# A two-layer SSD / linear-attention / retention trunk on one core: the SSD skip written into the output tiles by ACT, and a newly planned order

## The chip, the cores and the metric

The kernel runs on one core of one Trainium2 chip. The metric is the device time of one execution in microseconds; the number to predict is the median of three executions.

## The reference

One sequence of 1024 tokens, width 1024, passes through two layers. Each layer projects the residual stream once and splits the columns among three token mixers; their gated outputs are concatenated, projected, normalised and gated. All in fp32; cut to what matters here:

```python
for i in range(DEPTH):
    u = h @ w_in[i]                       # 3376 columns: z, xbc, dt, gla q/k/v/g/a, ret q/k/v/g
    # A) SSD: depthwise conv + silu on x, B, C; 8 heads of 64, state 128, both directions
    y = bidirectional(scalar_decay_scan, C, B, x*dt_f, x*dt_b, la_f, la_b)
    y = y + d_skip[:, None] * x           # the skip, one factor per head
    y_ssd = rms_norm(y * silu(z), norm_w)
    y_gla = gla_branch(...)               # B) gated linear attention, 4 heads
    y_ret = retention_branch(...)         # C) retention, 4 heads, rotary
    mix = concat(y_ssd, y_gla, y_ret) @ w_out[i]
    h = layer_norm(ALPHA * h + mix)
    h = h + sigmoid(h @ w_pg[i] + b_pg[i]) * (p[i] @ w_pe[i])
```

## The kernel before

**Dense products.** Activations lie as channels x tokens, in two halves of 512 tokens. Every dense operand is split into a high and a low part (names ending in hi/lo, h/l), and every dense product is three matmuls, hi*hi, hi*lo and lo*hi: `pch` (a 128-channel projection of the inputs), `ptk` (a projection with tokens on partitions: 304 columns at the start of a layer, 256 for retention's values, the stage `rvs`), `pout` (output projection), `ppg` and `ppe` (gate and embedding). A split is one ACT copy and one DVE subtraction (`whi`/`wlo` of input weights, `khi`/`klo` of the later ones).

**The mixers** run in chunks of 128 tokens, eight per layer and group. SSD has two groups of four heads. For each group it first runs backward over the chunks (`weighted`, `advance`: POOL scales x into `xw`, PE makes the state product `pst`, POOL scales the state into `sq`, DVE adds). Then `front` makes a chunk's decay matrix M in a tile `E` (a DMA, eight ACT operations, a DVE select, an ACT exp, a DVE product with the scores `psg`) and `back` uses it: `psi` (state times C), `dT<-psi,dT` on DVE, `xd` on POOL (both directions added), `psy` (x times M), and DVE adds `psy` and `xd` into the output tile `yz`. The skip sits in M: `dd`, a diagonal matrix with the heads' factors, is made once per group on POOL and added to each chunk's M by DVE (`E<-E,dd`), so that `psy` contains the skip. GLA (`gla1`): `pgr`, `bk`, `gqm`, `pgs` (scores), `gks`, `pkt`, `pgn` (states), `pgo` (values). Retention: `prk`, `prn`, then `prs`, `pro`. `yssd` normalises the SSD output: `pss` (transposes), a chain of small DVE operations, `psr`. `lnorm` is the layer norm, whose results are `h1h`/`h1l`.

**What sets the order.** The program is recorded, not issued: every call becomes a node with its dependencies, and `Rec.order` plans all engines together with prices from `Rec.price`, picking at each step the candidate that can start first (ties by recorded place). `Rec.issue` then emits every instruction from one line, L522, so rows of the profile are told apart by tile names. A resource `port` is kept in the plan: a DVE operation with two SBUF operands (or in a fast form) and any POOL operation exclude each other. DVE operations named in `EITHER` may be given to POOL when enough of them are late. The recorded order, which is the priority, comes from `weave`: the chains of the mixers (`phases`) with independent projections (`FILL`) mixed in by `QUOTA`. `SHIFTS` adds random offsets to the priorities of stretches of nodes, 21 of them. `DP` and `DB` say by how many chunks a front runs ahead of its back; `LN0`/`LN1` how the layer norm is spread over the projections.

Of the kernel before, what the change touches and what calls it, by code (L numbers as in the profile page):

```python
# [45 lines left out]
LN0=(2,2,2)  # L46
LN1=(4,1,2)
# [11 lines left out]
Q_N = 34 + 8 * 6  # L59
# [15 lines left out]
SHIFTS = (  # L75
# [6 lines left out]
EITHER = ("wlo", "klo", "yl", "rW", "rz", "gsm", "gqm", "gsq", "rsq")  # L82
LOOK = 20.0
# [141 lines left out]
class Rec:  # L225
# [93 lines left out]
    def price(self, eng, fn, args, kw, kind):  # L319
# [18 lines left out]
        if eng == "ACT":  # L338
            aps = sum(isinstance(kw.get(k), View) for k in ("scale", "bias"))
            c = .08 + n * .00082 + (0 if ps else .035) + .085 * aps  # L340
            return c, c + .1, False
        tensors = [v for v in ins if v.size > 1 or n == 1]
        if eng == "DVE":
            two = len(tensors) > 1 and not ps
            fast = fn in ("tensor_scalar", "tensor_copy") and not ps
            aps = sum(v.size == 1 for v in ins) if n > 1 else 0
            c = .07 + n / (1920 if fast else 960) + .06 * aps
            return c, c + .085, two or fast
# [5 lines left out]
    def order(self, nodes):  # L354
# [64 lines left out]
        while left:  # L419
            best = None  # L420
            for e in engines:
                cand, queue = None, ready[e]
                if e == "POOL":
                    now = max(at[e], port)
                    late = [n for n in ready["DVE"] if est[n.i] <= now]
                    queue = sorted(queue + [n for n in late[2:] if n.alt], key=prio)
# [23 lines left out]
                if cand is not None and (best is None or cand[0] < best[0]):  # L450
                    best = (*cand, e)
# [4 lines left out]
            t, _, n, e = best  # L456
# [69 lines left out]
def trunk(ctx: ExitStack, tc: tile.TileContext, xT, pT, wch, wt1, wt2, wout, wpg, wpe,  # L526
# [55 lines left out]
    def tt(eng, o, a, b, op):  # L582
        eng.tensor_tensor(o, a, b, op)
# [20 lines left out]
    FILL = 'c01dk2K3rQgGH'  # L604
    QUOTA = ((6, 8), (8, 17), (17, 22), (24, 28), (29, 35), (36, 36), (40, 40))
# [4 lines left out]
    GO = 1  # L610
    QF = 1
    DB = 2
    DP = (1,1,1,1)
# [174 lines left out]
    for layer in range(DEPTH):  # L788
# [87 lines left out]
        def conv_group(g):  # L876
            X[g] = [sl.get("X", (P, 2, 256)) for _ in range(4)]
            for i in range(2):
                xo = yield from conv(4 * g + i, lambda half, own: own)
                for half in range(2):  # L880
                    ps = cxt("pxt", (P, 4, P))
                    for c in range(4):
                        o = half * HALF + c * P
                        PX.transpose(ps[:, c, :], xo[:, o:o + P], ident)
                    for j in range(2):
                        act.activation(X[g][half * 2 + j][:, :, i * P:i * P + P],
                                       ps[:, 2 * j:2 * j + 2, :], AF.Copy)
                yield
# [13 lines left out]
        def ssd(g, B, C, Bt):  # L902
# [13 lines left out]
            def advance(dst, src, c, d, xw):  # L916
# [15 lines left out]
            dd = sl.get("dd", (P, 4, P))  # L932
            tt(pool, dd[:], ident.unsqueeze(1).broadcast_to([P, 4, P]),
               vb[:, 32 + 4 * g:36 + 4 * g].unsqueeze(2).broadcast_to([P, 4, P]), ALU.mult)

            def front(c):
# [22 lines left out]
                tt(vec_, M, M, dd[:], ALU.add)  # L959
                return M, xw, dT  # L960

            def back(c, Mx):
                M, xw, dT = Mx
                half, o = c // 4, slice((c % 4) * P, (c % 4 + 1) * P)
                if c % 4 == 0:
                    for j in range(2):
                        yz[2 * g + j][half] = sl.get("yz")
# [28 lines left out]
                for j in range(2):  # L996
                    tt(vec_, yz[2 * g + j][half][:, o], psy[:, j, :], u[:, j, :], ALU.add)
# [5 lines left out]
            sl.put(Sf, dd)  # L1003
# [703 lines left out]
```

## Time and profile before

| | us |
|---|---|
| median of 3 executions (lowest, highest) | 1247.55 (1246.6, 1248.52) |
| the profiled execution's own time | 1249.67 |
| its span, first to last instruction | 1247.9 |
| PE busy in the span | 1219.0 (98%) |
| DVE busy | 929.4 (74%) |
| ACT busy | 585.9 (47%) |
| POOL busy | 204.0 (16%) |

The profiled execution took 2.1 us more than the median, and 1.8 us of its time lie outside the span. PE was granted its full clock almost throughout (0.997 on the mean). A PE row's length is modelled: a dense matmul's row lasts 0.39 us though the next one starts 0.23 us later, so a wait shorter than the difference leaves no idle time in the rows.

### The profile page before, as it was taken

How to read it: one execution, taken by the hardware profiler on the slowest of the kernel's cores; microseconds unless marked ns; L12 is line 12 of the kernel's file. 1: busy time of each engine (PE TensorE's matmuls, PEld its weight loads, DVE VectorE, ACT ScalarE, POOL GpSimd, SP SyncE). 2: the span in 40 equal slices, each digit the busy share in tenths (PEclk: the TensorE clock that was granted, in tenths of full speed). 3: DMA queues.
4: the chain of work that ended last, by engine and by line, in shares of the span. 5: the costliest groups of instructions: out<-in, count | busy, mean ns of one | idle time of the engine just before them, and what ended most of it. 6: DMA issues, size and time to landing. Idle time of an engine off the chain costs nothing. (4 is left out here: it accounts for less than half of the span.)

```text
span 1247.9 us, 19871 instructions
## 1 busy us (share of the span) xinstructions
PE 1219.0 (98%) x7120; PEld 1009.2 (81%) x7120; DVE 929.4 (74%) x1982; ACT 585.9 (47%) x1237; POOL 204.0 (16%) x201
## 2 busy tenths in 40 slices
PE   8999999999999999999999999999999999999998
PEld 7887888768888788788898877787798887888887
DVE  5579897788588967796626788878686889579862
ACT  5466766532222435364534756565322224355552
POOL 0025552001001300120000354631000002001000
PEclk9999999999999999999999999999899999999999
DMA  7134432112132796233101453220121315952341
GB/s 252 43 98 154 147 123 76 43 33 70 48 102 66 236 309 219 85 125 132 65 28 51 151 149 126 86 93 18 46 66 43 101 53 198 340 183 85 118 157 51
DMA packets 82584, 142.58 MB, mean 114 GB/s; under 512 B 10867, under 2 KB 17973, under 8 KB 82485
## 3 DMA queue, kind: packets, MB, share of 16 engines
q1 hardware_dynamic: 82484, 141.31, 35.5%
q8 instruction: 56, 0.92, 0.3%
q14 instruction: 44, 0.35, 0.1%
HBM read 116.89 MB, written 17.04 MB: 107 GB/s over the span
## 5 line engine op out<-in xcount | busy, mean ns | idle before, releaser
L522 PE MATMUL pch<-xh,whi 128*128 128x512 f32 x352 | 147.1, 418 | 1.2 <-DVE gS L522 1.2
L522 PE MATMUL pch<-h2h,whi 128*128 128x512 f32 x352 | 145.8, 414 | 0.5 <-DVE E L522 0.5
L522 PE MATMUL pch<-xh,wlo 128*128 128x512 f32 x352 | 138.0, 392 | 0.1
L522 PE MATMUL pch<-h2h,wlo 128*128 128x512 f32 x352 | 137.8, 391 | 0.0
L522 PE MATMUL pch<-xl,whi 128*128 128x512 f32 x352 | 137.5, 391 | 0.0
L522 PE MATMUL pch<-h2l,whi 128*128 128x512 f32 x352 | 137.5, 391 | 0.0
L522 ACT ACTIVATE khi<-kraw 128x512 fp32r<-128x512 f32 (+1 forms) x160 | 89.1, 583 | 84.6 <-DMA kraw<-in_wout 40.8
L522 PE MATMUL ppg<-h1l,khi 128*128 128x512 f32 (+1 forms) x264 | 101.4, 384 | 1.8 <-DVE h1l L522 1.8
L522 PE MATMUL ppg<-h1h,khi 128*128 128x512 f32 (+1 forms) x264 | 101.1, 384 | 0.0
L522 PE MATMUL pout<-yl,khi 128*128 128x512 f32 x256 | 99.8, 390 | 1.0 <-DVE yl L522 1.0
L522 PE MATMUL ppg<-h1h,klo 128*128 128x512 f32 (+1 forms) x264 | 100.7, 383 | 0.0
L522 PE MATMUL pout<-yh,khi 128*128 128x512 f32 x256 | 100.7, 393 | 0.0
L522 PE MATMUL pout<-yh,klo 128*128 128x512 f32 x256 | 99.9, 390 | 0.7 <-DVE klo L522 0.7
L522 DVE SCALAR_TENSOR_TENSOR cacc<-cu,hp,cacc 128x1024 f32<-128x1024 f32 x64 | 87.8, 1372 | 16.2 <-ACT cacc L522 15.5
L522 DVE TENSOR_TENSOR wlo<-raw,whi 128x512 fp32r<-128x512 f32 (+1 forms) x79 | 56.7, 721 | 43.1 <-ACT whi L522 42.7
L522 ACT ACTIVATE whi<-raw 128x512 fp32r<-128x512 f32 (+1 forms) x98 | 60.8, 623 | 59.2 <-PE pch L522 39.6
L522 POOL TENSOR_TENSOR klo<-kraw,khi 128x512 fp32r<-128x512 f32 (+1 forms) x27 | 37.6, 1399 | 301.3 <-ACT khi L522 196.0
L522 ACT ACTIVATE E<-E,ecu 128x128 f32<-128x128 f32 x256 | 79.8, 392 | 8.5 <-DMA E<-dcu 8.4
L522 DVE TENSOR_TENSOR klo<-kraw,khi 128x512 fp32r<-128x512 f32 (+1 forms) x101 | 61.2, 622 | 29.6 <-ACT khi L522 13.0
L522 POOL TENSOR_TENSOR wlo<-raw,whi 128x512 fp32r<-128x512 f32 (+1 forms) x19 | 30.2, 1590 | 306.6 <-ACT whi L522 288.7
L522 PEld LDWEIGHTS pch<-xh,whi 128*128 128x128 f32 x352 | 66.2, 188 | 16.2 <-issue 3.6
L522 PEld LDWEIGHTS pch<-h2h,whi 128*128 128x128 f32 x352 | 66.2, 188 | 15.7 <-issue 1.9
(283 smaller groups left out, 2872.1 us busy)
## 6 DMA issues: line engine op xcount, KB each, us to landing
raw<-in_wch SPq DMA_DIRECT2D x88, 256.0 KB, 2.8
E<-dcu SPq DMA_DIRECT2D x32, 512.0 KB, 4.1
kraw<-in_wout SPq DMA_DIRECT2D x64, 256.0 KB, 4.2
kraw<-in_wpg SPq DMA_DIRECT2D x64, 256.0 KB, 3.2
dT<-deu SPq DMA_DIRECT2D x64, 128.0 KB, 3.4
dlo<-klo SPq DMA_DIRECT2D x32, 256.0 KB, 2.5
klo<-dlo SPq DMA_DIRECT2D x32, 256.0 KB, 4.3
xraw<-in_xT SPq DMA_DIRECT2D x16, 256.0 KB, 4.7
```

Of the source, the lines that this page charges most:

```text
L522: getattr(self.real[n.eng], fn)(*map(real, args), **{k: real(x) for k, x in kw.items()})
```

## The change

1. `dd` and `E<-E,dd` are gone. At the end of `conv_group` ACT writes `d_skip * x` into the output tiles `yz`, 128x512 at a time with a per-channel factor (new columns of `par` from Q_D); in `back` DVE adds twice, first `u` (the tile `xd` or `dT`), then `psy`, each 128x128.
2. The planner: `SHIFTS` is empty; ties between candidates that can start at the same moment go to the one that could ask for the port first; POOL is offered an `EITHER` operation when three others are late, not two; `LOOK` is 22; ACT and DVE operations on 64 partitions are priced higher.
3. The recorded order: another `FILL`, `QUOTA`, `GO`, `DB`, `DP`, `LN0`, `LN1`.

```diff
-LN0=(2,2,2)
-LN1=(4,1,2)
+LN0 = (4, 1, 2) 
+LN1 = (4, 2, 4) 
-SHIFTS = (
...
+SHIFTS = ()
-LOOK = 20.0
+LOOK = 22.0
+            if o.pn == 64 and n >= 128:
+                c += .1
...
-                    queue = sorted(queue + [n for n in late[2:] if n.alt], key=prio)
+                    queue = sorted(queue + [n for n in late[3:] if n.alt], key=prio)
...
-                if cand is not None and (best is None or cand[0] < best[0]):
-                    best = (*cand, e)
+                if cand is not None:
+                    asked = max(at[e], est[cand[2].i]) if cand[2].port else cand[0]
+                    if best is None or (cand[0], asked) < best[:2]:
+                        best = (cand[0], asked, *cand[1:], e)
...
-    FILL = 'c01dk2K3rQgGH'
-    QUOTA = ((6, 8), (8, 17), (17, 22), (24, 28), (29, 35), (36, 36), (40, 40))
+    FILL = 'c01kd2r3KQHGg'
+    QUOTA = ((6, 8), (13, 17), (20, 22), (27, 28), (27, 36), (36, 36), (36, 40))
...
-    GO = 1
+    GO = 0
-    DB = 2
-    DP = (1,1,1,1)
+    DB = 1
+    DP = (1, 2, 1, 1)
...
+                    y = yz[2 * g + i][half] = sl.get("yz")
+                    act.activation(y[:], xo[:, half * HALF:(half + 1) * HALF], AF.Copy,
+                                   scale=pr[:, Q_D + 2 * g + i:Q_D + 2 * g + i + 1])
...
-            dd = sl.get("dd", (P, 4, P))
-            tt(pool, dd[:], ident.unsqueeze(1).broadcast_to([P, 4, P]),
-               vb[:, 32 + 4 * g:36 + 4 * g].unsqueeze(2).broadcast_to([P, 4, P]), ALU.mult)
...
-                tt(vec_, M, M, dd[:], ALU.add)
...
-                    tt(vec_, yz[2 * g + j][half][:, o], psy[:, j, :], u[:, j, :], ALU.add)
+                    y = yz[2 * g + j][half][:, o]
+                    tt(vec_, y, y, u[:, j, :], ALU.add)
+                    tt(vec_, y, y, psy[:, j, :], ALU.add)
```

The set of PE instructions is the same in both, kind by kind; nearly every row stands elsewhere. In three places the prediction rests on the new order.

DVE in the second layer's second SSD group, near its end, before: a chunk's M gets the diagonal before `psy` can use it, and one addition per half of the chunk's channels ends the chunk.

```order
L522 TENSOR_TENSOR dT<-psi,dT 128x512
L522 COPY_PREDICATED E<-mki,E 128x512
L522 TENSOR_TENSOR yz<-psy,xd 128x128 x2
L522 TENSOR_TENSOR E<-E,psg 128x512
L522 TENSOR_TENSOR Sf<-sq,pst 128x256
L522 TENSOR_TENSOR E<-E,dd 128x512
```

The same place after:

```order
L523 TENSOR_TENSOR dT<-psi,dT 128x512
L523 TENSOR_TENSOR E<-E,psg 128x512
L523 TENSOR_TENSOR yz<-yz,xd 128x128
L523 TENSOR_TENSOR Sf<-sq,pst 128x256
L523 TENSOR_TENSOR yz<-yz,psy 128x128
L523 TENSOR_TENSOR yz<-yz,xd 128x128
L523 COPY_PREDICATED E<-mki,E 128x512
L523 TENSOR_TENSOR yz<-yz,psy 128x128
```

The 128x512 addition is gone, and two 128x128 additions have become four, two of which read SBUF alone.

PE in the second layer's GLA stage before, in its longest piece without a dense matmul:

```order
L522 MATMUL pkt<-kc,gks 128x128 x2
L522 MATMUL pgs<-gqm,bk 128x256 x3
L522 MATMUL pgn<-gv,gkt 128x128 x2
L522 MATMUL pgs<-gqm,bk 128x256 x4
L522 MATMUL pgr<-kc,gla 128x129 x2
L522 MATMUL pgo<-gv,gA 64x64 x8
```

The same stage after; the `ptk` rows go on to a piece of eleven to thirteen such matmuls before the next `pgn`:

```order
L523 MATMUL pgn<-gv,gkt 128x128 x2
L523 MATMUL pgo<-gv,gA 64x64 x8
L523 MATMUL pgs<-gqm,bk 128x256 x3
L523 MATMUL pkt<-kc,gks 128x128 x2
L523 MATMUL pgs<-gqm,bk 128x256
L523 MATMUL ptk<-wlo,h2h 128x256
L523 MATMUL ptk<-whi,h2l 128x256 x2
L523 MATMUL ptk<-whi,h2h 128x256
```

The projection of retention's values, which stood behind the stage, is now cut up inside it.

POOL from the end of the second layer's SSD on, before:

```order
L522 TENSOR_TENSOR wlo<-raw,whi 128x512
L522 TENSOR_TENSOR sq<-Sf,tot 128x256
L522 TENSOR_TENSOR wlo<-raw,whi 128x512
L522 TENSOR_TENSOR xd<-dT 128x256
L522 TENSOR_TENSOR gqm<-bk,kc 128x256 x8
L522 TENSOR_TENSOR gsm<-gS,kc 128x256 x3
```

And after:

```order
L523 TENSOR_TENSOR sq<-Sf,tot 128x256 x2
L523 TENSOR_TENSOR xd<-dT 128x256
L523 TENSOR_TENSOR gqm<-bk,kc 128x256 x2
L523 TENSOR_TENSOR wlo<-raw,whi 128x512
L523 TENSOR_TENSOR gqm<-bk,kc 128x256 x14
L523 TENSOR_TENSOR wlo<-raw,whi 128x512
L523 TENSOR_TENSOR klo<-kraw,khi 128x512 x7
```

All sixteen `gqm` of the layer are POOL's now. Over the program POOL takes 21 more `gqm`, 25 more `klo` of 512 and 9 of 256 columns, 10 more `wlo` and 2 more `yl`, and 2 `gsm` less: 130 operations that either engine could have taken, where it had 65.

## Rows read from the trace of the kernel before

**Rows 1.** The page: the span, and busy time of each engine with its share.

```profile
span 1247.9 us, 19871 instructions
...
PE 1219.0 (98%) x7120; PEld 1009.2 (81%) x7120; DVE 929.4 (74%) x1982; ACT 585.9 (47%) x1237; POOL 204.0 (16%) x201
```

**Rows 2.** Busy time by stretch, in the order length, PE, PEld, DVE, ACT, POOL, then granted clock and DMA: SSD and GLA of the first layer, SSD and most of GLA of the second.

```profile
104.00:208.00 104.00, 103.25 (x622) 83.23 (x621) 95.78 (x165) 71.01 (x175) 52.87 (x56) 1.00 0.41 127
208.00:312.00 104.00, 99.94 (x638) 80.21 (x637) 80.67 (x238) 41.27 (x99) 8.46 (x8) 1.00 0.18 49
676.00:832.00 156.00, 150.68 (x840) 120.87 (x839) 129.96 (x209) 104.25 (x249) 71.01 (x73) 1.00 0.37 118
832.00:884.00 52.00, 50.14 (x331) 37.58 (x331) 40.07 (x133) 24.96 (x69) 5.62 (x9) 0.93 0.09 27
```

**Rows 3.** Waits of PE over the whole program: those of the gate products for `h1l` (total us, times, longest).

```profile
PE ppg L522 <- DVE h1l L522: 1.8, 2, 1.1
```

**Rows 4.** Timeline, PE around 205 to 208 us (start, length): two dense matmuls that follow each other, and `psi` between dense ones.

```profile
205.41 0.40 PE L522 MATMUL pch<-xh,whi 128*128 128x512 f32 x1
...
205.64 0.39 PE L522 MATMUL pch<-xl,whi 128*128 128x512 f32 x1
...
207.24 0.39 PE L522 MATMUL pch<-xh,wlo 128*128 128x512 f32 x1
...
207.46 0.60 PE L522 MATMUL psi<-Cch,Sf 128*128 128x128 f32 x4
...
208.14 0.40 PE L522 MATMUL pch<-xl,whi 128*128 128x512 f32 x1
```

**Rows 5.** Instructions of four tiles in each layer, with ns min/median/max and the starts of the first and the last: `pst` and `psy` bound SSD, `pgr` and `pgo` GLA.

```profile
L522 PE MATMUL pst<-xw,Btk x56: 377/378/483, 90.7 to 197.4; 128*128 128x256 f32 x56
...
L522 PE MATMUL pst<-xw,Btk x56: 377/379/483, 705.5 to 821.2; 128*128 128x256 f32 x56
...
L522 PE MATMUL psy<-E,X x128: 272/273/323, 110.8 to 202.1; 128*64 128x128 f32 x128
...
L522 PE MATMUL psy<-E,X x128: 272/273/324, 728.1 to 828.4; 128*64 128x128 f32 x128
...
L522 PE MATMUL pgr<-kc,gla x32: 271/275/378, 214.7 to 243.5; 128*128 128x129 f32 x32
...
L522 PE MATMUL pgr<-kc,gla x32: 272/275/378, 841.0 to 862.4; 128*128 128x129 f32 x32
...
L522 PE MATMUL pgo<-gv,gA x128: 222/222/271, 234.6 to 270.7; 128*64 128x64 f32 x128
...
L522 PE MATMUL pgo<-gv,gA x128: 222/222/369, 855.5 to 886.7; 128*64 128x64 f32 x128
```

**Rows 6.** Groups of DVE instructions (busy us, mean ns of one, then idle before and its releaser).

```profile
L522 DVE TENSOR_TENSOR E<-E,dd 128x512 f32<-128x512 f32 x32 | 25.1, 792 | 0.1
...
L522 DVE TENSOR_TENSOR E<-E,psg 128x512 f32<-128x512 f32 x32 | 21.6, 679 | 2.2 <-ACT E L522 1.5 <-PE psg L522 0.5
...
L522 DVE TENSOR_TENSOR yz<-psy,xd 128x128 f32<-128x128 f32 x48 | 12.1, 280 | 2.6 <-POOL xd L522 2.5
```

**Rows 7.** The same for ACT and POOL.

```profile
L522 ACT ACTIVATE gt<-gt,pr 128x512 f32<-128x512 f32 x31 | 22.1, 721 | 23.8 <-DVE gt L522 23.7
...
L522 POOL TENSOR_TENSOR xw<-X,wtab 128x256 f32<-128x256 f32 x56 | 54.6, 980 | 20.8 <-PE pst L522 12.2 <-DVE wtab L522 8.2
...
L522 POOL TENSOR_TENSOR gqm<-bk,kc 128x256 f32<-128x256 f32 x10 | 6.6, 668 | 52.6 <-DVE bk L522 46.4 <-PE pgn L522 6.1
```

**Rows 8.** Timeline around 776 to 780 us, second layer's SSD: POOL, DVE and PE (in brackets the idle time before and its releaser).

```profile
776.02 1.74 POOL L522 TENSOR_TENSOR wlo<-raw,whi 128x512 fp32r<-128x512 f32 x1
...
776.55 2.30 DVE L522 SCALAR_TENSOR_TENSOR cacc<-cu,hp,cacc 128x1024 f32<-128x1024 f32 x1
...
779.37 0.40 DVE L522 TENSOR_TENSOR Sf<-sq,pst 128x256 f32<-128x256 f32 x1
...
779.83 0.71 PE L522 MATMUL psi<-Cch,Sf 128*128 128x128 f32 x4 [1.37 <-DVE Sf L522]
```

**Rows 9.** Timeline around 514 to 518 us, where the first layer's gate products begin.

```profile
513.79 0.63 PE L522 MATMUL psr<-dg,ones_r 128*128 128x512 f32 x2
...
517.15 3.63 DVE L522 SCALAR_TENSOR_TENSOR h1l<-res,pr,h1h 128x512 fp32r<-128x512 f32 x3
517.16 2.41 POOL L522 TENSOR_TENSOR klo<-kraw,khi 128x256 fp32r<-128x256 f32 x2 [2.79 <-PE ppe L522]
518.49 0.50 PE L522 MATMUL ppg<-h1l,khi 128*128 128x512 f32 x1 [1.10 <-DVE h1l L522]
```

**Rows 10.** Timeline from 393 to 405 us, first layer, `yssd`, and in the last row the two `psr` behind it (ns min/median/max, then the starts of first and last).

```profile
393.42 0.29 PE L522 MATMUL pro<-rv,rA 128*64 128x64 f32 x4
393.54 0.29 PE L522 MATMUL pro<-rS,rW 128*64 128x64 f32 x4
...
395.15 0.66 PE L522 MATMUL pss<-kc,zacc 128*128 128x128 f32 x4
...
404.37 1.30 POOL L522 TENSOR_TENSOR wlo<-raw,whi 128x304 fp32r<-128x304 f32 x1 [17.87 <-DVE w1l L522]
...
404.88 1.33 DVE L522 TENSOR_TENSOR dg<-kc,rl 128x512 fp32r<-128x512 f32 x1
...
L522 PE MATMUL psr<-dg,ones_r x2: 398/434/470, 407.8 to 408.1; 128*128 128x512 f32 x2
```

More of the change, by code (lines that the diff above doesn't have):

```diff
@@ L58 @@
 Q_SNW, Q_GNW, Q_RNW, Q_RNB, Q_LNW, Q_LNB, Q_BPG, Q_CONV = 0, 4, 6, 8, 10, 18, 26, 34
-Q_N = 34 + 8 * 6
+Q_D = 34 + 8 * 6
+Q_N = Q_D + 4
 K_ID, K_LE, K_GT, K_LT, K_UGF, K_UGB = 0, 128, 256, 384, 512, 641
@@ L347, in price @@
             c = .07 + n / (1920 if fast else 960) + .06 * aps
+            if o.pn == 64 and n >= 128:
+                c += .08
             return c, c + .085, two or fast
@@ L455, in order @@
             assert best is not None, [(e, len(r)) for e, r in ready.items()]
-            t, _, n, e = best
+            t, _, _, n, e = best
             if e != n.eng:
@@ L964, in back @@
                 half, o = c // 4, slice((c % 4) * P, (c % 4 + 1) * P)
-                if c % 4 == 0:
-                    for j in range(2):
-                        yz[2 * g + j][half] = sl.get("yz")
                 if YO == 0:
@@ L1002, in ssd @@
             yield from pipelined(range(NC), front, back, DP[0])
-            sl.put(Sf, dd)
+            sl.put(Sf)
         g0 = run(conv_group(0))
@@ L1673 @@
         cols += [conv[:, c - C_X:c - C_X + P].T for c in CONV_COLS]
+        cols.append(chan(np.repeat(a["d_skip"][l], 64)))
         pars.append(np.concatenate(cols, axis=1))
```

6 rows, old and new, of the table SHIFTS are left out of this document.

## The prediction

> **What bounds the kernel now.** I read the page first: PE is busy for 1219.0 of 1247.9 us [rows 1]. That share says little of how well PE works, since a dense matmul's row lasts 0.39 us and the next starts 0.23 us after it [rows 4]. What it does say is that PE sets the time. Both kernels issue the same matmuls, kind by kind, so only two things on PE can change: what it costs to go from one kind of matmul to another, and the waits.
>
> The first is about nothing. From 207.24 to 208.14 stand two dense matmuls and four `psi` passes [rows 4]: 0.90 us. Two dense pitches are 2 x 0.227 = 0.45, which leaves 0.11 per pass, and that is what the longer runs of `psi` take too. The new order goes from dense to other matmuls 181 times instead of 171; I cost the ten at zero.
>
> So the waits remain. PE's idle time is 28.9 us. The start of the program and the evacuation behind the last matmul stay as they are. What lies between I place by stretch: PE idles 0.8 of 104 us in the first layer's SSD and 4.1 of 104 around its GLA, but 5.3 of 156 in the second layer's SSD and 1.9 of 52 in its GLA [rows 2]. In the same stretches DVE is busy 92%, 78%, 83% and 77%; in SSD it is the engine that comes right behind PE.
>
> Idle rows hide the start of each wait, so I compare the two layers by the clock. SSD, from the first `pst` to the last `psy`, takes 202.1 - 90.7 = 111.4 us in layer 1 and 828.4 - 705.5 = 122.9 in layer 2 [rows 5]. The second holds 12 more dense matmuls (2.7 us), 18 more `pla` of half the columns (2.1) and two more `psi` (0.4). The other 6.3 us are waits that the first layer doesn't have. GLA, from the first `pgr` to the last `pgo`: 56.0 us with 108 dense matmuls among them, and 45.7 with 48. Less the dense part, 31.5 against 34.8: 3.3 us of waits more.
>
> **What makes PE wait.** Two places in the timeline show the same pattern. At 776.02 POOL begins `wlo` (1.74 us); DVE's `cacc`, begun half a microsecond later, takes 2.30 us; `Sf` behind it on DVE is late, and PE stands for 1.37 us before `psi` [rows 8]. At 517.16 POOL begins two `klo` (2.41 us), DVE's three `h1l` take 3.63 us, and PE waits for them 1.10 us and once more, 1.8 in all [rows 3, 9]. A DVE operation with two SBUF operands waits while POOL works. One that reads PSUM doesn't: `E<-E,psg` takes 0.679 us, while `E<-E,dd`, on the same tile, takes 0.792 on the mean [rows 6].
>
> **The change, part by part.**
>
> *The skip, on DVE.* Removed: 32 `E<-E,dd`, 25.1 us [rows 6]. The 64 old additions become 64 that read PSUM (0.28 each, as before) and 64 that read SBUF alone. For these no row exists. Below: 64 x 0.28 = 17.9 us [rows 6]. Above: each also waits half a POOL operation, 0.49 us by `xw` [rows 7], in the half of SSD's time that POOL is busy (52.87 of 104, [rows 2]): 0.25 more, 33.9 us. I take what contention added to `E<-E,dd`, 0.792 - 0.679 = 0.11: 64 x 0.39 = 25 us. DVE gains nothing, between -7 and +9. The path to `psy` loses 0.79 us per chunk, and `psy`'s PSUM tile no longer waits for POOL's `xd`, on which DVE waited 2.5 us in all [rows 6].
>
> The Trainium skill ("SBUF — State Buffer", section "Who interferes with whom") states that a DVE instruction with two SBUF inputs contends with a GpSimd one that reads SBUF, and that whoever comes first blocks the other fully. Rows 8 and 9 agree. By that rule the new additions stand in the worst place, right behind `xd`; the upper end would hold, DVE would have 9 us more, and SSD's gain below would be gone.
>
> *The skip, on ACT.* 16 operations at 0.72 us, by `gt<-gt,pr`, which also takes a per-channel operand [rows 7]: 11.5 us. ACT is busy 68% in SSD [rows 2], and nothing but the far later additions waits for them. Cost nothing; if that cover were gone, at most 11.5 us.
>
> *SSD's order.* Both layers now have one and the same order there, with 306 dense matmuls between first `pst` and last `psy` (282 and 294 before) and no `pla`. Best case: layer 2 does as layer 1, -6.3. Worst: layer 1 does as layer 2, +6.3. I start from zero, as the rows give no sign, and take half the best case, -3, for the shorter chain and the added cover.
>
> *GLA's order.* The stage now holds 12 dense matmuls and 142 (layer 2: 118) `ptk` of half the columns, 12 x 0.227 + 142 x 0.114 = 18.9 us of cover (16.2 in layer 2). Layer 1 had 24.5 and hardly waited, layer 2 10.9. With 16.2 I expect layer 2 to lose most of its 3.3 us: -3, between 0 and -3.3. `gqm`, at 0.67 us on POOL [rows 7], leaves DVE, but holds up those of DVE's operations beside it that read SBUF alone; I cost it below.
>
> *The gate products.* From `psr` at 513.79 to the first `ppg` that needs `h1l`, at 518.49, layer 1 had 4.7 us, 1.1 of it waiting [rows 9]: too short for DVE's `res` and `h1l`. In the new order 54 dense matmuls stand between them, 12.3 us. The wait of 1.8, 2.2 with its hidden start, goes: -2.
>
> *The SSD norm.* From `pss` to `psr` layer 1 took 12.65 us for 48 dense matmuls and the four `pss` themselves, 11.3 us: 1.3 late; of the last `dg`'s 1.33 us, 0.8 lay beside POOL's `wlo`, which began before it [rows 10]. In the new order stand there, in both layers, 30 dense (6.8 us), 64 `pro`, which are 128 passes at 0.12 per four (3.8) [rows 10], one `prs`, four transposes of the next tile and the `pss`, 0.3 to 0.45 each group: 11.8 us. That is half a microsecond more than layer 1 had. Late by 0.8 twice if the conflict comes again, hardly if not, where it was 1.3 once: 0, between -1.3 and +0.5.
>
> *POOL's load.* It had 65 operations that DVE could have done, and rows 3 and 8 to 10 give 1.4 + 1.8 + 0.8 = 4 us of PE waits that they caused. With 130 at the same rate, +4. But more than half of the new ones are `klo`, in output projection and gate products, where the planned order now leaves room, and the planner's new tie rule places the port's conflicts where the chip has them. I take +2, between 0 and +4.
>
> **Sum.** -3 - 3 - 2 + 0 + 2 = -6. The profiled execution had 1249.67 (1247.9 of span and 1.8 outside), so 1243.7 against it; it was 2.1 above the median, and the forecast for the median is 1247.55 - 6 = 1241.5 us.
>
> **Rivals.**
>
> *The order without shuffles is worse.* The 21 shuffled stretches may have carried layer 1's smooth SSD. Then both layers run as layer 2 did: +6.3 in SSD, GLA unchanged, -2 and +2 as above: 1247.55 + 6.3 = 1254; half of it gives 1251. It decides once SSD in layer 1, less its dense matmuls and `pla`, takes more than about 50 us (111.4 - 64.0 - 0.7 = 47 now, 53 in layer 2). For it: nothing else explains why one stage differs so between layers. Against it: layer 2 lay inside the shuffled ranges too. Chance 0.12.
>
> *The port.* POOL's time grows by up to 21 x 0.67 + 35 x 1.74 + 9 x 1.2 = 86 us [rows 7 to 9], and each of the 64 new SBUF additions can be held up. If only a tenth of these 64, and as many of the 31 new `gqm` and `wlo`, end in a PE wait like that of rows 8 (1.4 us), that is 9 x 1.4 = 13 us against the 8 gained: 1252. It decides from six such waits on. The chance is from the rows, which show three such places for 65 operations: 0.12. The rule of the Trainium skill quoted above would have it wherever POOL comes first, and gives no rate.
>
> *Nothing moves.* Each wait gone is taken up by the next one, since DVE carries the same load in SSD (above): 1245 to 1250. Chance 0.16.
>
> *All waits in the mixers go.* Idle 12 us in the four stretches of [rows 2], some 16 with hidden starts; two thirds of it and the -2: 1235. Chance 0.12.
>
> *The forecast,* -2.5 to -9.5 us: 0.48.
>
> **Range and chances.** A change under 0.2%, 2.5 us, can't be told from none here. Faster 0.48 + 0.12 = 0.60, same 0.16, slower 0.24. The range from 1234 to 1252 leaves out the deeper part of the gain and the worse half of the two losses, some 0.2; the forecast's own is 1238 to 1245.
>
> **What would show it.** In the changed profile SSD of both layers should take about 306 x 0.227 + 47 to 49 = 116 to 118 us from first `pst` to last `psy`; GLA, less its cover, 31 to 32 us in both; no wait of `ppg` for `h1l` in layer 1. `yz<-yz,xd` should take 0.3 to 0.5 us, and `yz<-yz,psy` 0.28. The forecast is wrong if layer 1's SSD loses what layer 2's wins, or if PE's waits end at DVE operations stretched beside a POOL row.

## The result, and the profile after

The changed kernel took 1219.89 us (1219.69 to 1220.42), the kernel before beside it 1247.69: a ratio of 0.9777, 95% interval 0.9764 to 0.9789. That is 27.8 us less, where 6 were forecast. The sign was right; the time lies far below the range.

The page after, its span, busy times and granted clock:

```profile
span 1218.0 us, 19959 instructions
...
PE 1202.9 (99%) x7120; PEld 1006.3 (83%) x7120; DVE 917.0 (75%) x1949; ACT 591.0 (49%) x1253; POOL 264.3 (22%) x262
...
PEclk9999999999999999999999999999999999999999
```

Against [rows 1], PE is busy for 16.1 us less with the same 7120 rows, and idle for 15.1 us, where it was 28.9. So more than half of the gain isn't idle time in PE's rows.

All waits of PE that are left (total us, times, longest):

```profile
PE ptk L523 <- ACT xh L523: 6.1, 3, 4.7
PE pkt L523 <- DVE gks L523: 1.5, 4, 1.0
PE ppg L523 <- ACT gt L523: 0.9, 1, 0.9
PE prk L523 <- DVE rot L523: 0.8, 1, 0.8
PE pout L523 <- DVE yl L523: 0.7, 1, 0.7
```

The first is the start of the program. The wait for `h1l` of [rows 3] is gone. The last is of the kind of [rows 8, 9]: `yl` on DVE, 0.68 us at its median, takes 1.77 beside a `wlo` that POOL began half a microsecond earlier, and `pout` waits for it.

```profile
427.10 1.74 POOL L523 TENSOR_TENSOR wlo<-raw,whi 128x512 fp32r<-128x512 f32 x1
427.62 1.77 DVE L523 TENSOR_TENSOR yl<-glay,yh 128x512 fp32r<-128x512 f32 x1
429.44 0.50 PE L523 MATMUL pout<-yl,khi 128*128 128x512 f32 x1 [0.71 <-DVE yl L523]
```

Where did the time go? Between four marks both kernels do the same work: the first `pst` and the first `pout` of each layer. Before, `pout`, layer 1 and layer 2 (ns min/median/max, then starts of the first and the last):

```profile
L522 PE MATMUL pout<-yh,khi x128: 389/389/481, 420.0 to 511.7; 128*128 128x512 f32 x128
...
L522 PE MATMUL pout<-yh,khi x128: 389/389/494, 1040.4 to 1137.1; 128*128 128x512 f32 x128
```

After, `pst`, `psy`, `pgr`, `pgo` and `pout` of layer 1, then of layer 2:

```profile
L523 PE MATMUL pst<-xw,Btk x56: 377/378/483, 91.9 to 198.4; 128*128 128x256 f32 x56
...
L523 PE MATMUL psy<-E,X x128: 272/273/324, 109.7 to 205.4; 128*64 128x128 f32 x128
...
L523 PE MATMUL pgr<-kc,gla x32: 271/274/277, 229.3 to 262.2; 128*128 128x129 f32 x32
...
L523 PE MATMUL pgo<-gv,gA x128: 222/222/271, 239.8 to 276.2; 128*64 128x64 f32 x128
...
L523 PE MATMUL pout<-yh,khi x128: 388/389/481, 409.7 to 502.3; 128*128 128x512 f32 x128
...
L523 PE MATMUL pst<-xw,Btk x56: 377/378/483, 692.9 to 799.5; 128*128 128x256 f32 x56
...
L523 PE MATMUL psy<-E,X x128: 272/273/324, 710.7 to 806.4; 128*64 128x128 f32 x128
...
L523 PE MATMUL pgr<-kc,gla x32: 271/274/378, 830.4 to 863.5; 128*128 128x129 f32 x32
...
L523 PE MATMUL pgo<-gv,gA x128: 222/222/270, 840.9 to 875.6; 128*64 128x64 f32 x128
...
L523 PE MATMUL pout<-yh,khi x128: 389/389/481, 1010.8 to 1102.1; 128*128 128x512 f32 x128
```

With the `pst` starts of [rows 5]:

| stretch (same work in both) | before | after | |
|---|---|---|---|
| start to first `pst` | 90.7 | 91.9 | +1.2 |
| mixers of layer 1, `pst` to `pout` | 329.3 | 317.8 | -11.5 |
| output projection and gate, to the next `pst` | 285.5 | 283.2 | -2.3 |
| mixers of layer 2 | 334.9 | 317.9 | -17.0 |
| to the end | 207.5 | 207.2 | -0.3 |

Both layers' mixers now take the same time, and layer 1's, which I had taken as the smooth ones, lost 11.5 us. Inside the mixers I use the prediction's measure, a stage less its cover (0.227 us per dense matmul, 0.114 per half-width `ptk`, 0.12 per `pla`), and call it the stage's rest. SSD before: 46.7 and 53.3 us; after, with 306 dense matmuls in 113.5 us, 44.0 and 44.0. GLA before: 31.5 and 34.8; after 46.9 - 18.9 = 28.0 and 45.2 - 16.2 = 29.0. The measure leaves small kinds in the rest: before, eight `pga` (0.11 us each) stood in each layer's SSD stretch and now none does, and layer 1's has four `psi` more (0.11 each). So of the 2.7 and 9.3 us that SSD's rest lost, some 2.3 and 8.4 are SSD's own.

The same four stages by window (length; PE, PEld, DVE, ACT, POOL; clock; DMA), as [rows 2]: PE doesn't idle in SSD, and the clock is 1.00 everywhere; [rows 2] had 0.93 in layer 2's GLA.

```profile
91.90:205.40 113.50, 113.50 (x659) 92.57 (x657) 99.57 (x181) 80.37 (x200) 65.90 (x68) 1.00 0.42 127
229.30:276.20 46.90, 45.55 (x421) 38.66 (x422) 40.35 (x125) 24.27 (x72) 11.33 (x17) 1.00 0.09 24
692.90:806.40 113.50, 113.50 (x657) 92.38 (x657) 99.64 (x181) 80.07 (x199) 63.92 (x68) 1.00 0.42 127
830.40:875.60 45.20, 44.88 (x403) 37.11 (x401) 38.09 (x126) 24.41 (x73) 11.39 (x17) 1.00 0.09 25
```

The skip's own operations after, on DVE and ACT (busy us, mean ns, idle before), for [rows 6, 7]:

```profile
L523 DVE TENSOR_TENSOR yz<-yz,xd 128x128 f32<-128x128 f32 x48 | 18.4, 400 | 5.2 <-POOL xd L523 5.2
...
L523 DVE TENSOR_TENSOR yz<-yz,psy 128x128 f32<-128x128 f32 x64 | 16.6, 277 | 0.7
...
L523 DVE TENSOR_TENSOR yz<-yz,dT 128x128 f32<-128x128 f32 x16 | 5.9, 377 | 0.2
...
L523 ACT ACTIVATE yz<-cacc,pr 128x512 f32<-128x512 f32 x16 | 11.1, 716 | 1.5 <-DVE cacc L523 1.5
```

The mean of 400 ns hides two kinds: 34 of the 48 `yz<-yz,xd` took 0.30 us or less, the other 14 took 0.68 to 0.72. Each of the 14 began while a POOL operation was running, and ended 0.15 us after that operation's row. One of them, with its `sq`:

```profile
131.48 0.61 POOL L523 TENSOR_TENSOR sq<-Sf,tot 128x256 f32<-128x256 f32 x1
131.55 0.69 DVE L523 TENSOR_TENSOR yz<-yz,xd 128x128 f32<-128x128 f32 x1 [0.90 <-POOL xd L523]
```

### The profile page after: what moved, and what is told of

Read it like the earlier page. It is cut to its first block, busy times and chain, and to the rows that moved or that the text cites. A ratio compares the mean times of both kernels' runs of the same rounds, so it can differ in the third digit from the quotient of the medians.

```text
span 1218.0 us, 19959 instructions
## 1 busy us (share of the span) xinstructions
PE 1202.9 (99%) x7120; PEld 1006.3 (83%) x7120; DVE 917.0 (75%) x1949; ACT 591.0 (49%) x1253; POOL 264.3 (22%) x262
## 4 chain that ended last, share of the span: by engine, by line
PE 92%; DVE 5%; DMA 1%; issue 1%; ACT 1%; SPq 0%; DVEq 0%; ACTq 0%
PE pch L523 37%; PE ppg L523 14%; PE pout L523 13%; PE ptk L523 8%; PE ppe L523 4%; PE psi L523 2%; PE pst L523 2%; PE psy L523 2%; PE pro L523 1%; PE pgs L523 1%; PE prs L523 1%; DVE rt L523 1%; PE psg L523 1%; PE prn L523 1%; DVE gks L523 1%
## 5 line engine op out<-in xcount | busy, mean ns | idle before, releaser
L523 POOL TENSOR_TENSOR klo<-kraw,khi 128x512 fp32r<-128x512 f32 (+1 forms) x61 | 76.5, 1272 | 303.4 <-ACT khi L523 111.2
L523 POOL TENSOR_TENSOR wlo<-raw,whi 128x512 fp32r<-128x512 f32 (+1 forms) x29 | 44.7, 1546 | 365.9 <-ACT whi L523 271.2
L523 ACT ACTIVATE khi<-kraw 128x512 fp32r<-128x512 f32 x160 | 89.1, 582 | 54.9 <-DMA kraw<-in_wout 26.5
L523 DVE SCALAR_TENSOR_TENSOR cacc<-cu,hp,cacc 128x1024 f32<-128x1024 f32 x64 | 92.1, 1438 | 12.7 <-ACT cacc L523 11.5
L523 PEld LDWEIGHTS pch<-xh,wlo 128*128 128x128 f32 x352 | 66.1, 188 | 14.5
L523 PEld LDWEIGHTS pch<-h2h,wlo 128*128 128x128 f32 x352 | 66.1, 188 | 14.4
## 6 DMA issues: line engine op xcount, KB each, us to landing
raw<-in_wch SPq DMA_DIRECT2D x88, 256.0 KB, 2.9
kraw<-in_wout SPq DMA_DIRECT2D x64, 256.0 KB, 4.6
kraw<-in_wpg SPq DMA_DIRECT2D x64, 256.0 KB, 3.1
dlo<-klo SPq DMA_DIRECT2D x32, 256.0 KB, 4.0
klo<-dlo SPq DMA_DIRECT2D x32, 256.0 KB, 4.6
xraw<-in_xT SPq DMA_DIRECT2D x16, 256.0 KB, 5.1
```

The source lines that it names most:

```text
L523: getattr(self.real[n.eng], fn)(*map(real, args), **{k: real(x) for k, x in kw.items()})
```

## The experiments

The change has four separable parts: shuffles out, skip on ACT, planner rules, order. I added them one at a time to the kernel before without its shuffles, undid them one at a time in the changed kernel, and then cut the larger ones up. "Clock" is the mean granted clock of the profiled execution.

| kernel | median us | ratio to before (95%) | clock |
|---|---|---|---|
| before | 1247.69 | 1 | 0.997 |
| b_noshuf: before, no shuffles | 1281.7 | 1.025 (1.0222 to 1.0278) | 0.981 |
| b_reseed: before, fresh seeds | 1278.76 | 1.0254 (1.0217 to 1.0291) | 0.990 |
| b_skip: b_noshuf and the skip | 1274.84 | 1.0206 (1.0187 to 1.0226) | 0.986 |
| b_plan: b_noshuf and the planner rules | 1258.93 | 1.0075 (1.0047 to 1.0103) | 0.988 |
| b_order: b_noshuf and the order | 1246.33 | 0.9982 (0.997 to 0.9994) | 0.994 |
| b_pairs: before, `pgs`/`prs` in one piece | 1270.53 | 1.0161 (1.0125 to 1.0197) | 0.985 |
| changed | 1219.89 | 0.9777 (0.9764 to 0.9789) | 0.999 |
| a_dd: skip undone | 1223.36 | 0.9796 (0.977 to 0.9822) | 0.998 |
| a_oldplan: planner rules undone | 1238.4 | 0.9917 (0.9899 to 0.9936) | 0.999 |
| a_unasked: tie rule alone undone | 1233.55 | 0.9874 (0.9848 to 0.99) | 0.997 |
| a_oldorder: order undone | 1253.3 | 1.0044 (1.0031 to 1.0058) | 0.995 |
| a_oldfill: FILL, QUOTA, GO undone | 1240.16 | 0.9934 (0.9918 to 0.9951) | 0.996 |
| a_oldssd: DB, DP undone | 1231.76 | 0.9868 (0.9854 to 0.9883) | 0.994 |
| a_oldln: LN0, LN1 undone | 1233.27 | 0.9882 (0.9868 to 0.9897) | 0.995 |
| a_shuf: old shuffles put in | 1245.41 | 0.9974 (0.9961 to 0.9987) | 0.993 |
| a_look: LOOK 21 | 1222.32 | 0.9793 (0.9778 to 0.9808) | 1.0 |
| a_split: row halves in another order | 1224.46 | 0.9801 (0.9775 to 0.9827) | 0.997 |
| a_pairs: `pgs`/`prs` in one piece | 1215.23 | 0.9723 (0.9692 to 0.9754) | 0.999 |

The intervals of a_dd, a_look and a_split overlap that of the changed kernel, so their 2.4 to 4.6 us aren't clear of noise by themselves; b_skip's touches that of b_noshuf.

**The parts, added one at a time.** b_noshuf is the kernel before with `SHIFTS = ()`; the others add one item of the change to it: b_skip all of item 1, b_plan item 2 without LOOK, b_order item 3 and LOOK.

```diff
-SHIFTS = (
...
+SHIFTS = ()
```

> The kernel before with the table of shuffled stretches emptied and nothing else. Four theories share the 27.8 us between the two kernels. If the shuffles were the harm (theory S), this alone gives 1228 to 1235. If they were a tuned gain (my rival in the prediction) it is slower, 1250 to 1256. If the gain comes from the planner's rules (P), the skip (K) or the stage order (O), this one stays within 1244 to 1252.

> The kernel before without shuffles, and the skip written by ACT: against the run without shuffles it is the skip alone. Theory K (a 0.79 us operation less in each chunk's path on a nearly full DVE): 8 to 15 us less than that run, all of it in SSD. My prediction's term: 3 us less at most. The port theory (64 new SBUF additions held up by POOL): 0 to 5 us more.

> The kernel before without shuffles, with the planner's new tie rule, the threshold of three late operations and the price of 64-partition operations: the planner's part alone. Theory P (conflicts at the shared port are now foreseen): 10 us or more below the run without shuffles, and fewer DVE operations stretched beside POOL in front of a PE wait. The other theories: within 4 us of it.

> The kernel before without shuffles, with the new FILL, QUOTA, GO, DB, DP, LN0, LN1 and LOOK: the stage order alone. Theory O (dense cover inside GLA and in front of the gate products): 8 to 15 us below the run without shuffles, in GLA, retention and the start of the gate products, with SSD as it was. My prediction's terms for these gave 5. The other theories: within 4 us.

Without shuffles 33.4 us are lost (against 1248.28 of the kernel before beside it). Alone, the skip then gives 6.9, the planner rules 22.8, the order 35.4. The sum, 33.4 - 65.1 = -31.7, is near the 27.8 measured. So the small step that I forecast is a large loss and a larger gain, and I had priced neither near its size. In b_noshuf part of the loss is the clock. One window (columns as above, clock third from the end):

```profile
242.70:263.20 20.50, 20.50 (x92) 13.61 (x94) 14.04 (x48) 7.36 (x21) 1.53 (x2) 0.50 0.06 14
```

And PE in the timeline there (start, length, idle before and releaser):

```profile
242.25 0.41 PE L516 MATMUL pkt<-kc,gks 128*128 128x128 f32 x2 [1.57 <-DVE gS L516]
...
248.87 0.63 PE L516 MATMUL pch<-xh,wlo 128*128 128x512 f32 x1
249.30 0.63 PE L516 MATMUL pch<-xh,whi 128*128 128x512 f32 x1
```

After a wait of 1.57 us PE is granted the lower level (0.50, 1.2 of 2.4 GHz); dense matmuls then start 0.43 us apart instead of 0.227. By the mean clock all such stretches of b_noshuf cost up to (0.997 - 0.981) x 1282 = 20 us against the kernel before, more than half of the loss; this is an estimate, which takes PE for the limit in them. The four kernels of this group differ by 0.013 in clock, some 17 us; so the skip's 6.9 us, with 0.005 of clock between (6 us), is hardly more than clock.

**The parts, undone one at a time.** The edits are parts of the change, reversed: a_dd puts back `dd`, `E<-E,dd` and the one addition per half; a_oldplan has the old tie rule, threshold and prices; a_oldorder the old tables and `LOOK`; a_shuf the old `SHIFTS`. Of each one line:

```diff
+                tt(vec_, M, M, dd[:], ALU.add)
...
-                    queue = sorted(queue + [n for n in late[3:] if n.alt], key=prio)
+                    queue = sorted(queue + [n for n in late[2:] if n.alt], key=prio)
...
-    FILL = 'c01kd2r3KQHGg'
+    FILL = 'c01dk2K3rQgGH'
...
-SHIFTS = ()
+SHIFTS = (
```

> The changed kernel with the diagonal of the skip put back into the decay matrix on DVE, and one addition per half chunk again; new order, new planner rules, no shuffles. If the parts add up, the skip is worth what it was worth on the kernel without shuffles, -6.9 us: about 1227. If the skip matters only by how the planner happens to fall (the seven were clock, not work): anywhere from 1215 to 1230, with the same number of E and yz operations and no row showing the skip as the cause. If the diagonal really stands on the way to psy, SSD alone should lose 0.1 to 0.2 us per chunk, 3 to 6 us over 32 chunks, and the rest of the program should lie still.

> The changed kernel with the old planner rules (tie by recorded place, POOL offered an operation when two are late, no surcharge for 64 partitions); LOOK stays at 22. If the parts add up: 1220 + 22.8 = 1243. If the rules helped only because the kernel without shuffles was a bad plan, less: 1222 to 1230. My own prediction held them for worth at most 2 us: 1222. [...]

> The changed kernel with the old FILL, QUOTA, GO, DB, DP, LN0, LN1 and LOOK. If the parts add up: 1220 + 35.4 = 1255. If order and planner rules repair the same waits, so that one of them is enough: 1225 to 1240. The runs without shuffles had 24 us from PE's lower clock level; if that is what the order is worth, low stretches of some 20 us or more should stand here again.

> The changed kernel with the 21 shuffled stretches of the kernel before, which were found for another order. If shuffles as such shorten the plan: faster than 1220. If they helped only where they were fitted to the order of before: no better, and more likely 5 to 20 us slower, 1225 to 1240. My rival in the prediction (the order without shuffles is worse) would have this one faster by up to 6 us.

The skip is worth 3.5 us by the medians (2.4 by the ratios, and not clear of noise), but the profile has it in SSD, as expected: its rest is 45.7 and 45.6 us with the diagonal (116.5 and 119.1 us with 312 and 324 dense), +1.7 and +1.6. The planner rules are worth 18.5, the order 33.4, each somewhat less than alone. The low clock that I expected from the undoing of the order is not what that costs: 0.995 against 0.999 is 5 us of 33. The shuffles made for the old order cost 25.5 us in the new one.

**Shuffles with other seeds.** The edit adds 100000 to each of the 21 seeds.

```diff
-    (7056, 4761, 5061, 150), (9183, 3470, 3770, 20), ...
+    (107056, 4761, 5061, 150), (109183, 3470, 3770, 20), ...
```

> The kernel before with the same 21 shuffled stretches, the same widths and other seeds, nothing else. The kernel without shuffles took 1281.7, 33 us more than before. If shuffling as such loosens a bad order: near 1248. If only these 21 draws, kept because each fitted, carry the 33 us: as the kernel without shuffles or worse, 1275 to 1300. The changed kernel lost 25 us under shuffles made for another order, which speaks for the second.

1278.76: not told apart from no shuffles at all. As far as one other set of seeds can show, these draws carry the 33 us, and not shuffling as such.

**The planner's part.** a_unasked undoes the tie rule alone.

```diff
-                if cand is not None:
-                    asked = max(at[e], est[cand[2].i]) if cand[2].port else cand[0]
-                    if best is None or (cand[0], asked) < best[:2]:
-                        best = (cand[0], asked, *cand[1:], e)
+                if cand is not None and (best is None or cand[0] < best[0]):
+                    best = (*cand, e)
```

> The changed kernel with the old tie rule alone (recorded place instead of who could ask for the port first); POOL's threshold and the 64-partition prices stay new. If the tie rule is what the planner's part is worth: most of the 18.5 us, 1234 to 1239. If POOL's threshold or the prices carry it: 1220 to 1226. If any disturbance of the plan costs: somewhere from 1225 to 1240, with no more DVE time beside POOL than in the changed kernel.

13.7 of the 18.5 us; the other 4.8, of threshold and prices, I didn't take apart. It is also this rule that moves work to POOL; a_unasked's busy times:

```profile
PE 1210.5 (98%) x7120; PEld 1008.0 (82%) x7120; DVE 925.1 (75%) x2030; ACT 594.9 (48%) x1253; POOL 165.5 (13%) x181
```

POOL has 181 instructions and not 262; all kernels here with the old tie rule have 181 to 201, all with the new one 258 to 277. The time shows in GLA and SSD; GLA of layer 1 in a_unasked:

```profile
L521 PE MATMUL pgr<-kc,gla x32: 271/275/378, 232.9 to 272.1; 128*128 128x129 f32 x32
...
L521 PE MATMUL pgo<-gv,gA x128: 222/222/369, 250.8 to 281.2; 128*64 128x64 f32 x128
```

48.3 us, with 6 dense and 107 `ptk` among them (13.5): a rest of 34.8 against 28.0, up to half of the difference by a clock of 0.50 from 256.0 to 262.8 us. In layer 2 it is 31.2 against 29.0, in SSD 46.8 and 46.7 against 44.0: 14.5 us in the four stages, about all of it. Whether the rule gains by the work it takes off DVE or by the conflicts that it foresees, these runs don't separate.

**The order's parts.** One group of tables is undone in each of three kernels (a_oldln, a_oldssd, a_oldfill); the fourth, a_look, changes a number of the planner that stands for nothing.

```diff
-LN0 = (4, 1, 2) 
-LN1 = (4, 2, 4) 
+LN0=(2,2,2)
+LN1=(4,1,2)
...
-    DB = 1
-    DP = (1, 2, 1, 1)
+    DB = 2
+    DP = (1,1,1,1)
...
-    QUOTA = ((6, 8), (13, 17), (20, 22), (27, 28), (27, 36), (36, 36), (36, 40))
+    QUOTA = ((6, 8), (8, 17), (17, 22), (24, 28), (29, 35), (36, 36), (40, 40))
...
-LOOK = 22.0
+LOOK = 21.0
```

> The changed kernel with the old LN0 and LN1 alone, which say how the layer norm's products and its h1h/h1l are spread over the output projection and the embedding. In the kernel with the whole old order the stretch from pss to the last ppg lost 6.7 us in layer 1 and 8 in layer 2 against my count of PE's work, in the changed one 1.6 and 2. If that is LN0 and LN1: +8 to +13, 1228 to 1233, with ppg waiting for h1h or h1l again. If it is the stages ahead: within 3 us of 1220.

> The changed kernel with the old DB and DP alone (how far a front runs ahead of its back in SSD). If the lead of the fronts is what smooths SSD: the 5 to 12 us that SSD loses with the old order, 1225 to 1232, and all of it between the first pst and the last psy. If SSD is smooth through the cover by projections: within 3 us of 1220.

> The changed kernel with the old FILL, QUOTA and GO (which projections stand beside which mixer, and when GLA's outputs are made). If cover is the order's worth: the larger part of its 33 us, +15 to +25, 1235 to 1245, in GLA and retention and in SSD of layer 2. If the three groups of the order add up to 33, this one and the two others will have sums near it; if each alone costs as much as all, any disturbance of this plan does.

> The changed kernel with LOOK 21 instead of 22, a change of the planner's view that stands for no part of the diff: a disturbance without a meaning. If the parts carry the gain and the plan is robust: within 3 us of 1220. If the gain lies in one plan that was found among many, this costs about as much as the undoing of the parts does, 8 to 20 us.

LN0 and LN1 are worth 13.4 us. a_oldln's waits:

```profile
PE ppg L523 <- ACT h1h L523: 3.2, 2, 1.6
...
PE ppg L523 <- DVE h1l L523: 1.4, 3, 0.7
```

Those 4.6 us are a third of it; the stretches of output projection and gate take 290.8 and 213.6 us instead of 283.2 and 207.2, a clock of 0.82 from 1105 to 1124 us among it (up to 3.4 us). DB and DP are worth 11.9. SSD of layer 1 in a_oldssd:

```profile
L523 PE MATMUL pst<-xw,Btk x56: 377/378/483, 91.6 to 207.8; 128*128 128x256 f32 x56
...
L523 PE MATMUL psy<-E,X x128: 272/273/324, 111.2 to 214.7; 128*64 128x128 f32 x128
```

123.1 us with 312 dense: a rest of 52.3, in layer 2 51.8, so 8 us per layer more in SSD, a few of which the stages behind win back. Of the 16 us in both layers the eight `pga`, which stand in each stretch again, make 1.8, and 6.8 us at a clock of 0.50 in each (from 171.2 and from 778.8) up to 6.8; some 7.5 are left for the fronts. FILL, QUOTA and GO are worth 20.3. The profiled execution, at 1243.75 the slowest of the four, has 13 us more in SSD (a rest of 51.8 and 49.0 with 264 dense) and 3 in GLA. Of the 13, again 1.8 are `pga`, and up to 3.4 a stretch at 0.50 in layer 1: its mean clock was 0.996, and 0.998 to 0.999 in the other three. The three add to 45.5 where all together cost 33.4: partly the same waits, and a table undone alone stands beside others that were not chosen with it. But not every disturbance costs that much: LOOK 21 puts another tile on 1221 of the 7120 places in PE's order, the undoing of DB and DP on 1409, and LOOK 21 costs 2.4 us.

**Neighbours on PE.** In the changed kernel's timeline, `pgs`, whose operands stand on 64 of PE's 128 rows, two of a chunk's four on the upper half and two on the lower (each matmul is two passes, x2):

```profile
240.42 1.13 PE L523 MATMUL pgs<-gqm,bk 64*128 64x256 f32 x6
241.48 0.44 PE L523 MATMUL pkt<-kc,gks 128*128 128x128 f32 x2
241.85 0.70 PE L523 MATMUL pgs<-gqm,bk 64*128 64x256 f32 x2
242.47 0.39 PE L523 MATMUL ptk<-wlo,xh 128*128 128x256 f32 x1
```

Three take 1.06 us and one alone 0.62, 1.68 for the chunk's four. a_pairs and b_pairs plan the four `pgs`, and the two `prs`, as one piece:

```diff
                 key = (id(args[0].mem), kind[0])
+                if args[0].mem.name in ("pgs", "prs"):
+                    key = args[0].mem.name
...
-                n.deps, n.after, n.mems, n.prio, n.kind = set(), [], set(), i + bias, kind
+                n.deps, n.after, n.mems, n.prio, n.kind = set(), [], {}, i + bias, kind
...
-                    n.mems.add(m)
+                    n.mems[m] = True
```

The last lines keep a node's tiles in the order in which they were met.

> The changed kernel with the four pgs and the two prs of a chunk planned as one piece. It has 22.3 us for pgs now, and groups of four at 1.06 us would be 17: up to 5 us faster, 1215, if the rest of the plan holds. If any disturbance of this plan costs time, as the shuffles did (1245), slower by 5 to 20 us.

> The kernel before, with the four pgs (and the two prs) of a chunk planned as one piece, so that nothing comes between them; shuffles, skip and order as before, though the plan around them shifts. If adjacency is worth what the two profiles suggest (pgs 30.0 to 22.3 us, prs 14.6 to 10.4), 8 to 12 us faster than before, less what the shuffles lose by no longer fitting. If the loss of the fit weighs as much as in the kernel without shuffles, up to 25 us slower. In both cases the time from pgs to the next row should come to about 1.06 us for four.

a_split swaps the loops of `pgs`, and in the same way those of `prs`:

```diff
-                for d in range(2):
-                    for i, r in enumerate((UP, DN)):
+                for i, r in enumerate((UP, DN)):
+                    for d in range(2):
```

> The changed kernel, where the score products pgs and prs of a chunk are recorded as upper, upper, lower, lower row half instead of upper, lower, upper, lower; nothing else differs, and the operations and operands are the same. If two neighbours on different halves of PE's rows run side by side, as a group of four in 1.06 us against about 1.25 for two pairs of one half suggests, 64 pgs and 64 prs lose their partners in part: 4 to 12 us slower, with pgs and prs rows dearer and the rest still. If neighbours mean nothing and only waits count: within 2 us of 1220.

In a_pairs:

```profile
240.52 1.13 PE L525 MATMUL pgs<-gqm,bk 64*128 64x256 f32 x8
241.58 0.44 PE L525 MATMUL pkt<-kc,gks 128*128 128x128 f32 x2
```

Four take the 1.06 us that three took. From the start of each to the next matmul's, all `pgs` take 17.6 us instead of 22.3 and all `prs` 9.5 instead of 10.4: 5.6 us, of which 4.7 arrive. At 1215.23 a_pairs is the fastest kernel here. On the kernel before the same edit makes `pgs` cheaper too (30.0 to 20.0) and loses 22 us, up to 15 of them by the clock (0.985 against 0.997). That the shuffles' index ranges no longer meet what they were drawn for is a likely reason, which no run isolates.

a_split refutes only a part of my mechanism. With the halves in the order upper, upper, lower, lower a group of four `pgs` takes 1.07 us just the same. But two `prs` of one half, which this edit leaves by themselves in six places, take 0.64 us, and two of different halves in the changed kernel 0.42 (from their start to that of the next row; a_split first):

```profile
366.74 0.71 PE L523 MATMUL prs<-rW,rot 64*128 64x128 f32 x4
367.38 0.50 PE L523 MATMUL pch<-xh,whi 128*128 128x512 f32 x1
```

```profile
375.83 0.49 PE L523 MATMUL prs<-rW,rot 64*128 64x128 f32 x4
376.25 0.34 PE L523 MATMUL pro<-rv,rA 128*64 128x64 f32 x4
```

So in these rows two matmuls of one piece run side by side when they stand on different halves, whatever their order, and two on one half don't. In a_split `prs` rose from 10.4 to 12.3, and `pout` waits 5.4 us for `glay`, while `pgs` fell to 18.5 (the planner keeps two calls that write one tile together, so this edit glued them as well); in all it was 4.6 us slower. What counts is that a piece holds as many of one half as of the other.

The rows of `pgs` (busy, mean ns), before, changed, and a_pairs:

```profile
L522 PE MATMUL pgs<-gqm,bk 64*128 64x256 f32 x128 | 27.8, 445 | 1.2 <-DVE bk L522 0.4 <-ACT gS L522 0.4 <-DVE gqm L522 0.4
```

```profile
L523 PE MATMUL pgs<-gqm,bk 64*128 64x256 f32 x128 | 23.0, 408 | 0.0
```

```profile
L525 PE MATMUL pgs<-gqm,bk 64*128 64x256 f32 x128 | 18.6, 402 | 0.1
```

## Why the prediction was right or wrong

**"What it costs to go from one kind of matmul to another ... is about nothing."** Wrong for two kinds, though little of this change's gain. I measured it on `psi` between dense matmuls [rows 4] and took it for all kinds. For `pgs` and `prs` it isn't so: one alone costs as much as two. Start to start, `pgs` fell from 30.0 to 22.3 us and `prs` from 14.6 to 10.4, 11.9 of the 29.9 us that the span lost. But most of these 11.9 are waits, and the clock, that fall between these rows. Before, `pgs` stood in 12 pieces of one or two, 10 of three or four and 3 of five or six; after, in 7 and 16. At 0.63, 1.06 and 1.49 us a piece (undisturbed ones; 1.49 is an estimate, one step of 0.43 more) that is 22.6 and 21.4 us. `prs`, priced in the same way, comes to 11.3 and 10.4. So the new order won about 2 us of this price; how much was left in it a_pairs shows, 4.7 us.

**"So the waits remain", measured by comparing the two layers.** This step set the bound of my best case (1235) and failed most. I had waits of 6.3 and 3.3 us in layer 2 and hardly any in layer 1; the mixers lost 17.0 and 11.5. A comparison of layers sees only what one has and the other has not; layer 1 held 11.5 us of loss of its own. Of the span's 29.9 us, 13.8 are idle time of PE, up to 3.4 a stretch at half the clock (below), about 2 the neighbours above; the other ten or so, the hidden starts of waits among them, I haven't taken apart. A measure that might have shown it was in my hands: dense matmuls at 0.227 and the other kinds at the pitch of their undisturbed runs, summed over the program.

**The skip.** Right in its parts: the additions that read SBUF took 18.4 + 5.9 = 24.3 us (25 forecast), the others 277 ns (280), ACT 11.1 us (11.5), and no wait of PE ends at it. My upper end, 33.9, would have added 16 us to 17.9; the trace has 6.4. The rule of the Trainium skill ("SBUF — State Buffer", section "Who interferes with whom"), that whoever comes first blocks the other fully, I read as giving that upper end. The trace agrees with the rule where POOL had begun first, 0.68 us and more against 0.28, but that was so for only 14 of the 48 `yz<-yz,xd`. The skip's gain, 3.5 us, is as much as the whole -3 in SSD that I gave the shorter chain and the added cover together.

**SSD's order, -3.** Right in sign, a quarter of the size: its rest fell by 2.7 and 9.3, 12.0 in all, some 10.7 of it SSD's own (113.5 us from `pst` to `psy`, where 116 to 118 were to show the forecast right). I started from zero "as the rows give no sign"; the lead of the fronts (a_oldssd) and the cover (a_oldfill), some 7.5 us of rest each without `pga` and the clock, are what I gave no price, and the 6.3 that I read from [rows 5] was no bound.

**GLA's order, -3.** 3.5 + 5.8 = 9.3; the stage less its cover takes 28 to 29 us, not 31 to 32. 7.7 of them stand in the rows of `pgs`, most of them waits and clock. And the 3.3 us more of layer 2 that I called waits are, by the estimate below, the clock's: behind the 0.93 of [rows 2] stands this window of the kernel before,

```profile
876.30:883.10 6.80, 6.80 (x37) 4.88 (x36) 5.37 (x18) 2.49 (x8) 1.23 (x2) 0.50 0.01 1
```

6.8 us at 0.50, with PE busy throughout: 3.4 of them lost. I had read the 0.93 and drawn nothing from it.

**Gate products, -2, and the norm, 0.** The wait for `h1l` is gone and the stretch from `pout` to the next `pst` is 2.3 us shorter: right. LN0 and LN1 carry 13 us in the new order, but not in this comparison: the kernel before was nearly as good in these stretches without them (285.5 and 207.5 us; 287.4 and 213.3 in b_noshuf, up to 5 us of that by the clock). The norm's stretch, `pss` to `psr`, stayed (about 12.7 us before, 12.9 after), so zero was right. In the rest of the mixers 28.5 - 12.0 - 9.3 = 7.2 us were won that I had no term for; 4 of them stand in the rows of `prs`.

**POOL's load, +2.** Wrong in sign, as far as load and rule can be priced together. The 130 operations come with the tie rule; I counted the load as a cost and took the rule as something that softens it. Together they give 14 us, and of PE waits of the kind of [rows 8, 9] one is left, the 0.7 us for `yl`. What the load costs by itself no run shows.

**The shuffles, a rival at +6.3.** Right that they carried a gain, wrong in place and size. Their removal costs 33 us, but SSD's rest grows by only 2.8 in layer 1, to 49.4, under the 50 that I had named as the sign, and by 3.6 in layer 2. The loss isn't the difference of the two layers; up to 20 us of it are the clock. I priced their removal in one sum with the new order; alone, the two are prices of 33 and -35, and the net of -6 came from neither.

## What to carry to other kernels

Price a reordering against the pure work of the bounding engine (count times undisturbed pitch of each kind), not against its recorded waits or a smoother sibling stage. Offsets that were drawn for one plan were a loss in the next (a_shuf), and an edit that is good in another plan lost under them (b_pairs): take them out before you change the order. That new draws would pay again wasn't tried. Short matmuls on half of PE's rows belong together in pairs, one on each half.

## What the hardware showed that was not expected

A `pgs` on 64 of 128 rows takes 0.62 us alone and 0.63 us with a second one, of the other half, beside it; three or four take 1.06, four in either order of the halves. Two `prs` take 0.42 us on different halves and 0.64 on one. The 14 slow `yz<-yz,xd`, DVE additions of two SBUF operands, each ended 0.15 us after the POOL row that had begun before them. After most of the waits of PE named here, of one to two microseconds, the granted clock stood at 0.50 for stretches of several microseconds, in which dense matmuls start 0.43 us apart; the changed kernel, with 99% of PE busy, has none between the start and its last evacuation, and the kernel before one of 6.8 us. Whether the clock falls at a given wait isn't settled by these runs: the changed kernel waits 1.0 us for `gks` once without it, and the kernel before 1.37 us at 779.83 [rows 8]; in a_dd it stood at 0.50 for 3.4 us from 223.7, and no wait of PE of 0.15 us or more lies in the six microseconds before.
